# Moving the bias and cache loads, and the stores of new keys and values, from SyncE's DMA queue to GpSimd's, in a two-layer streaming encoder kernel

## The chip, the cores and the metric

The kernel runs on one core of one Trainium2 chip. The core has five engines with a queue of instructions each: TensorE (PE, with its weight loads as PEld), VectorE (DVE), ScalarE (ACT), GpSimd (POOL) and SyncE (SP), and 16 DMA engines that all queues share. An engine starts its instructions in the order in which they are written; an instruction that waits holds up everything behind it on that engine. A DMA is started by an instruction in the queue of some engine. The metric is the device time in microseconds (us) of one execution, the median of several runs.

## What is computed

Two groups of frames share the weights: 256 frames of a new stream and 64 frames that continue an old one. Cut to what matters:

```python
for l in range(DEPTH):                                   # DEPTH = 2
    qa, ka, va, qb, kb, vb, qi, ki, wi = project(x, w_in[l], pos)
    oa = band_attention(qa, ka, va, cache_a_k[l], cache_a_v[l], rel_bias[l])   # bias by clipped distance
    ob = sparse_attention(qb, kb, vb, qi, wi, ki, cache_b_k[l], cache_b_v[l], cache_b_kidx[l])
    x = layer_norm(ALPHA * x + concat(oa, ob) @ w_out[l])
    x = layer_norm(ALPHA * x + relu(x @ w_up[l]) ** 2 @ w_down[l])
# returned: x, and the new ka, va, kb, vb, ki of each layer
```

## The kernel before

All activations lie transposed, features on the partitions and the 320 frames along the row. Each product of fp32 matrices is made of three matmuls on split operands (high by high, high by low, low by high): the helper `mm3`, lines 188 to 190 of the profile. A weight block of 128 by 1024 numbers, a *unit*, is loaded in pairs of 1 MB into one of two `raw` buffers (`load_raw`, L151), split by ACT into its high part `wh` (L170) and by DVE into the low part `wl` (L176). When the second unit of a pair is split, `split_rest` calls `need_raw`, which writes the load of the pair after the next.

The order of the instructions of each engine is fixed in the program: a list of delayed calls (`later`, `advance`, with the delays of the table `WAIT`) decides where attention work stands among the matmuls, and nothing is rescheduled behind it.

In the projection part of a layer, each head pair gets a `Pair` object. Where it is of band A, `bias_tiles` loads its bias first: per head one load of 128x128, one of 128x256 (`bp[h]`) and one of 64x320 (`bs`), all L341; after each head two POOL memsets (L342, L343) mask corners of the tile just loaded, and so wait for the first two of these loads to land. Then `Pair.__init__` clears a piece of the value tile (L364, POOL) and loads cached keys and values (L367, L368). For the sparse branch `Index` loads its cached keys once per layer (L483).

POOL also prepares the queries of the continued stream: `sample_blocks` (L351 copy, L352 and L353 memsets), called when a query has been projected. TensorE's score matmuls for the continued stream read that tile: L535 for the indexer (`dots`), L396 for attention (`scores`). They stand in TensorE's order among the projection matmuls, so what makes them wait makes every matmul behind them wait.

New keys and values are stored to DRAM right after they are computed: `o_ka` (L771), `o_kb` (L308), `o_va` and `o_vb` (L317), `o_ki` (L499). All loads and stores are in SP's queue.

Of the kernel before, what the change touches and what calls it, by code (L numbers as in the profile page):

```python
# [69 lines left out]
def encoder_step(ctx: ExitStack, tc: tile.TileContext, a: dict):  # L70
    nc = tc.nc
# [19 lines left out]
    def main_acc():  # L91
        return acc("mm", 8 - N_SIDE)
# [4 lines left out]
    def side_banks(n, fn, *args):  # L97

        if held[0] + n > N_SIDE:
            later(NEXT, fn, *args)  # L100
            return None
        held[0] += n
        return [acc("at", N_SIDE) for _ in range(n)]

    def release(n):
        held[0] -= n

    def unit(dt=F32, w=T):
        return st([P, 3 * P], "u", N_UNIT, dt)[:, :w]
# [8 lines left out]
    def later(dt, fn, *args):  # L118
        agenda.append((clock[0] + dt, len(agenda), fn, args))
# [161 lines left out]
    def evacuate(dst, src, scale=1.0):  # L281
        s, b = src
        if b is None:
            nc.scalar.activation(dst, s, AF.Copy, scale=scale)
        elif scale != 1.0:
            nc.vector.tensor_scalar(dst, s, b, scale, op0=ALU.add, op1=ALU.mult)
        else:
            nc.scalar.activation(dst, s, AF.Identity, bias=b, scale=scale)

    def swap(dst, src):  # L290
        for q in range(4):
            nc.scalar.activation(dst[32 * q:32 * q + 32], src[32 * (q ^ 1):32 * (q ^ 1) + 32], AF.Copy)  # L292

    def rotate(t, f, sw, c):
        nc.vector.tensor_tensor(t, f, rope[:, c], op=ALU.mult)
        nc.vector.tensor_tensor(sw, sw, rope[:, c + 1], op=ALU.mult)
        nc.vector.tensor_tensor(t, t, sw, op=ALU.add)

    def roped(t, src, c, out, then):

        f, sw = unit(), unit()
        evacuate(f, src)
        swap(sw, f)

        def turn():
            rotate(t, f, sw, c)
            if out is not None:
                nc.sync.dma_start(out, t)  # L308
            then()

        later(WAIT[l]["rope"], turn)

    def value(v, src, out, then):

        f = unit()
        evacuate(f, src)
        nc.sync.dma_start(out, f)  # L317

        def turn():
            got = side_banks(1, turn)  # L320
            if not got:
                return
            pt = got[0]
            release(1)
            for c, n in ((0, P), (1, P), (2, TS)):
                nc.tensor.transpose(pt[:n, c * P:(c + 1) * P], f[:, c * P:c * P + n], ident)
            nc.scalar.activation(v[:, 0:2], pt[:, 0:2 * P].rearrange("p (c d) -> p c d", c=2), AF.Copy)
            nc.scalar.activation(v[:TS, 2], pt[:TS, 2 * P:3 * P], AF.Copy)
            then()

        later(WAIT[l]["value"], turn)

    def bias_tiles(l, j):

        e = a["rel"]
        bp, bs = [unit(w=3 * P) for _ in range(2)], unit()
        for h in range(2):
            off = e.offset + (l * 8 + 2 * j + h) * N_DIST
            for dst, at0, n, m in ((bp[h][:, 0:P], 192, P, P), (bp[h][:, P:], 64, P, 2 * P),
                                   (bs[64 * h:64 * h + 64], 0, TS, NKEY)):  # L340
                nc.sync.dma_start(dst, bass.AP(tensor=e.tensor, offset=off + at0, ap=[[1, n], [1, m]]))  # L341
            nc.gpsimd.memset(bp[h][64:P, 64:P], NEG)  # L342
            nc.gpsimd.memset(bp[h][64:P, 5 * 64:6 * 64], NEG)  # L343
        return bp, bs
# [10 lines left out]
    class Pair:  # L355


        def __init__(self, l, br, j, add):
            self.qf, self.k, self.v = unit(w=3 * P), unit(), unit(w=3 * P).rearrange("p (c d) -> p c d", c=3)
            self.o = unit(F32R), unit(F32R)  # L360
            self.flip = br == "a"
            self.q = self.qf[:, 64:] if self.flip else self.qf[:, :T]
            self.qs = self.qf[:, :P] if self.flip else self.qf[:, 2 * P:]
            nc.gpsimd.memset(self.v[TS:, 2], 0.0)  # L364
            self.add = add
            self.kc, self.vc = unit(w=PAST), unit(w=PAST).rearrange("p (c d) -> p c d", c=2)
            nc.sync.dma_start(self.kc, a["kc" + br][l, j])  # L367
            nc.sync.dma_start(self.vc, a["vc" + br][l, j])  # L368
            self.cols = (slice(192, T), slice(64, 192), slice(0, 64)) if self.flip else (
                slice(0, P), slice(P, 2 * P), slice(TP, T))  # L370
            self.have = set()
            self.done = False
# [58 lines left out]
        def turn(self):  # L431
            banks = side_banks(3, self.turn)
            if not banks:
                return
            release(3)
            self.pt = []
            for h, (p, t) in enumerate(zip((*self.sp, self.ss), banks)):
                pt = unit(w=3 * P)
                if h == 2:
                    nc.gpsimd.memset(pt[TS:, 2 * P:], 0.0)  # L440
                for c, n in ((0, P), (1, P), (2, P if h < 2 else TS)):
                    nc.tensor.transpose(t[:n, c * P:(c + 1) * P], p[:, c * P:c * P + n], ident)  # L442
                if h < WAIT[l]["pa" if self.flip else "pb"]:
                    nc.vector.tensor_copy(pt, t[:, :3 * P])
                elif h < 2:
                    nc.scalar.activation(pt, t[:, :3 * P], AF.Copy)
                else:
                    nc.scalar.activation(pt[:, :2 * P], t[:, :2 * P], AF.Copy)
                    nc.scalar.activation(pt[:TS, 2 * P:], t[:TS, 2 * P:3 * P], AF.Copy)
                self.pt.append(pt)  # L450
            self.got("p")
# [23 lines left out]
    class Index:  # L475


        def __init__(self, l):
            self.l = l
            self.qf = [unit(w=3 * P) for _ in range(4)]  # L480
            self.q = [q[:, :T] for q in self.qf]
            self.kx = unit(w=PAST)
            nc.sync.dma_start(self.kx, a["kidx"][l])  # L483
            self.mask = []
            self.k = self.w = None
            self.weighed = 0
# [9 lines left out]
        def turn(self):  # L496
            self.k = unit()
            rotate(self.k, self.kd, self.sw, 0)
            nc.sync.dma_start(a["o_ki"][self.l], self.k[0:64])  # L499
            self.weights()  # L500

        def weights(self):
# [246 lines left out]
    for l in range(DEPTH):  # L749
# [4 lines left out]
        def take(name, j, src):  # L754
            if name == "ki":
                index.keys(src)
            elif name == "qi":
                roped(index.q[j], src, 0, None, lambda: index.got(j))
            else:
                p, kind, br = pairs[name[1], j], name[0], name[1]  # L760
                if kind == "v":
                    value(p.v, src, a["o_" + name][l, j], lambda: p.got("v"))
                elif br == "b":
                    roped(getattr(p, kind), src, 2 if kind == "q" else 0, a["o_kb"][l, j] if kind == "k" else None,
                          lambda: p.got(kind))
                elif kind == "q":
                    evacuate(p.q, (src[0][:, T - 1::-1], src[1]), scale=HD ** -0.5)
                    later(WAIT[l]["a"] - WAIT[l]["scores"] if kind == "k" else 0, p.got, kind)
                else:
                    evacuate(p.k, src)  # L770
                    nc.sync.dma_start(a["o_ka"][l, j], p.k)  # L771
                    later(WAIT[l]["a"] - WAIT[l]["scores"] if kind == "k" else 0, p.got, kind)

        uses = []
        for s, (name, j) in enumerate(W_IN_ORDER[l]):
            br = name[1]
            if name[1] in "ab" and (br, j) not in pairs:
                pairs[br, j] = Pair(l, br, j, bias_tiles(l, j) if br == "a" else index.mask)
            uses.append(partial(take, name, j))
            if l > 0 or s > 0:  # L780
                project(base + s + 1 - len(uses), l > 0 and s < N_DEFER, *uses)
                uses = []
# [12 lines left out]
        for m in range(KD):  # L795
            if m < N_OUTER:
                p = accs[m]
            else:
                prefetch(wo + m + AHEAD)
                p = main_acc()  # L800
# [26 lines left out]
        for m in range(KD):  # L827
            if m % 2 == 0:
                later(2.0, before.apply, m)
            p = main_acc()  # L830
# [102 lines left out]
```

## Time and profile before

| | us |
|---|---|
| median of 3 runs | 839.5 (838.03 to 839.92) |
| the profiled execution | 836.99 |
| its span, first to last instruction | 835.2 |
| TensorE busy | 821.1 |
| VectorE busy | 594.6 |
| ScalarE busy | 494.0 |
| GpSimd busy | 28.7 |
| mean granted TensorE clock | 0.993 of full speed |

The span is the time from the first to the last instruction of the profiled execution; 1.8 us of its own time lie around it. "Busy" counts work of an engine, not the issuing of DMAs, which stands under the name of the queue (SPq). A granted clock of 1.00 is TensorE's 2.4 GHz, 0.50 its 1.2 GHz.

### The profile page before, as it was taken

Reading aid. Unit: us, or ns where it says so; the run is one execution under the profiler, and the core shown is the slowest. Engines: PE = TensorE matmul, PEld = TensorE weight load, DVE = VectorE, ACT = ScalarE, POOL = GpSimd, SP = SyncE. Lnnn points to the kernel's source line nnn. Section 1 sums busy time; section 2 is a strip of 40 time slices with the busy share of each in tenths; the row PEclk is TensorE's granted clock in tenths of the full one; section 3 lists DMA queues with packets and bytes.
Section 4 is the critical chain, followed back from the end, with each engine's and each line's share of the span. In section 5 each row is a group of like instructions: output and inputs, shape, how many; then the busy total and the mean of one; then the engine's idle time right before and its main releaser. Section 6 shows DMA issues by size and latency. Waiting matters only on the chain.

```text
span 835.2 us, 15008 instructions
## 1 busy us (share of the span) xinstructions
PE 821.1 (98%) x5792; PEld 794.3 (95%) x5792; DVE 594.6 (71%) x1284; ACT 494.0 (59%) x955; POOL 28.7 (3%) x145
## 2 busy tenths in 40 slices
PE   9979999999999999999998999999999999999997
PEld 7969999999999999999998989999999999999995
DVE  5649878586998883545496679996699888545343
ACT  6846798565665553434358977885556655434332
POOL 0110000000000000000000010110000000000000
PEclk9999999999999999999999999999999999999998
DMA  8676343343444444534687324342334444434411
GB/s 275 192 191 180 135 143 126 125 151 103 151 156 147 152 154 149 177 127 155 194 171 261 108 101 135 120 177 74 136 145 151 152 151 152 160 144 152 151 51 64
DMA packets 35033, 124.05 MB, mean 149 GB/s; under 512 B 6033, under 2 KB 21521, under 8 KB 22290
## 3 DMA queue, kind: packets, MB, share of 16 engines
q1 hardware_dynamic: 34962, 123.10, 44.6%
q8 instruction: 46, 0.75, 0.4%
q14 instruction: 25, 0.20, 0.1%
HBM read 116.36 MB, written 6.72 MB: 147 GB/s over the span
## 4 chain that ended last, share of the span: by engine, by line
PE 75%; DVE 10%; ACT 8%; DMA 4%; SPq 1%; issue 1%; ACTq 0%; DVEq 0%
PE mm L188 23%; PE mm L189 23%; PE mm L190 23%; DMA raw<-w_all 4%; DVE wl L176 2%; ACT u L292 2%; ACT wh L170 2%; ACT u L418 1%; DVE u L577 1%; PE at L442 1%; DVE m L575 1%; PE at L394 1%; DVE u L410 1%; PE at L461 1%; PE at L396 1%
## 5 line engine op out<-in xcount | busy, mean ns | idle before, releaser
L188 PE MATMUL mm<-u,wh 128*128 128x320 f32 (+1 forms) x1048 | 328.8, 314 | 0.3 <-ACT wh L227 0.2
L190 PE MATMUL mm<-u,wl 128*128 128x320 f32 (+1 forms) x1048 | 324.0, 309 | 0.4 <-DVE wl L176 0.3
L189 PE MATMUL mm<-u,wh 128*128 128x320 f32 (+1 forms) x1048 | 323.8, 309 | 0.2 <-DVE u L233 0.2
L170 ACT ACTIVATE wh<-raw 128x1024 fp32r<-128x1024 f32 x199 | 209.5, 1055 | 182.9 <-PE mm L189 108.4
L176 DVE TENSOR_TENSOR wl<-raw,wh 128x1024 fp32r<-128x1024 f32 x199 | 241.3, 1217 | 57.8 <-ACT wh L170 57.3
L188 PEld LDWEIGHTS mm<-u,wh 128*128 128x128 f32 (+1 forms) x1048 | 196.8, 188 | 2.1 <-ACT wh L227 1.0
L190 PEld LDWEIGHTS mm<-u,wl 128*128 128x128 f32 (+1 forms) x1048 | 196.5, 187 | 1.6 <-DVE wl L228 0.9
L189 PEld LDWEIGHTS mm<-u,wh 128*128 128x128 f32 (+1 forms) x1048 | 196.9, 188 | 0.4 <-DVE u L233 0.4
L188 PE MATMUL mm<-rh,wh 128*128 128x322 f32 x568 | 177.5, 313 | 0.0
L190 PE MATMUL mm<-rh,wl 128*128 128x322 f32 x568 | 176.2, 310 | 0.0
L189 PE MATMUL mm<-rl,wh 128*128 128x322 f32 x568 | 175.8, 310 | 0.0
L189 PEld LDWEIGHTS mm<-rl,wh 128*128 128x128 f32 x568 | 107.2, 189 | 0.2
L188 PEld LDWEIGHTS mm<-rh,wh 128*128 128x128 f32 x568 | 107.1, 189 | 0.2
L190 PEld LDWEIGHTS mm<-rh,wl 128*128 128x128 f32 x568 | 106.5, 188 | 0.0
L603 DVE SCALAR_TENSOR_TENSOR x<-x,mm 128x320 f32<-128x320 f32 x31 | 15.0, 487 | 78.9 <-PE mm L190 78.9
L292 ACT ACTIVATE u<-u 32x320 f32<-32x320 f32 x104 | 48.7, 469 | 1.8
L270 DVE SCALAR_TENSOR_TENSOR z<-mu,mm 128x320 f32<-128x320 f32 x71 | 38.7, 545 | 12.7 <-PE mm L190 12.7
L811 ACT ACTIVATE z<-z,c 128x320 f32<-128x320 f32 x64 | 35.8, 560 | 16.8 <-DVE z L272 15.8
L418 ACT ACTIVATE u<-u,mx 128x128 f32<-128x128 f32 (+2 forms) x80 | 37.0, 464 | 8.9 <-DVE mx L413 8.9
L605 ACT ACTIVATE rh<-x,ln 128x320 fp32r<-128x320 f32 x24 | 13.5, 563 | 45.4 <-DVE x L603 45.4
L818 DVE TENSOR_TENSOR u<-h,u 128x320 fp32r<-128x320 f32 x64 | 31.5, 492 | 7.2 <-DVE h L817 0.5
L272 DVE TENSOR_TENSOR z<-z,rstd 128x320 f32<-128x320 f32 x71 | 34.9, 492 | 0.0
(135 smaller groups left out, 710.4 us busy)
## 6 DMA issues: line engine op xcount, KB each, us to landing
raw<-w_all SPq DMA_DIRECT2D x99, 1024.0 KB, 4.8
u<-rel SPq DMA_DIRECT2D x16, 128.0 KB, 5.5
u<-rel SPq DMA_DIRECT2D x16, 80.0 KB, 5.8
o_va<-u SPq DMA_DIRECT2D x8, 160.0 KB, 5.3
o_ka<-u SPq DMA_DIRECT2D x8, 160.0 KB, 2.3
o_kb<-u SPq DMA_DIRECT2D x8, 160.0 KB, 1.8
o_vb<-u SPq DMA_DIRECT2D x8, 160.0 KB, 1.8
o_y<-x SPq DMA_DIRECT2D x8, 160.0 KB, 1.9
```

What stands on the lines that cost most here:

```text
L170: nc.scalar.activation(hi, w, AF.Copy)
L176: nc.vector.tensor_tensor(lo, w, hi.bitcast(F32), op=ALU.subtract)
L188: nc.tensor.matmul(out, hi[:, k], xh, start=first, stop=False)
L189: nc.tensor.matmul(out, hi[:, k], xl, start=False, stop=False)
L190: nc.tensor.matmul(out, lo[:, k], xh, start=False, stop=last)
L270: nc.vector.scalar_tensor_tensor(u, mu[:n], p[:, T:T + 1], p[:, :T], op0=ALU.mult, op1=ALU.add)
L272: nc.vector.tensor_tensor(u, u, rstd[:n], op=ALU.mult)
L292: nc.scalar.activation(dst[32 * q:32 * q + 32], src[32 * (q ^ 1):32 * (q ^ 1) + 32], AF.Copy)
L418: nc.scalar.activation(p, p, AF.Exp, bias=self.mx[:, i:i + 1], scale=1.0, accum_out=self.sums[:, i:i + 1])
L603: nc.vector.scalar_tensor_tensor(r, r, ALPHA, psum, op0=ALU.mult, op1=ALU.add)
L811: nc.scalar.activation(u, u, AF.Relu, bias=b)
L818: nc.vector.tensor_tensor(hl, h, hh.bitcast(F32), op=ALU.subtract)
```

## The change

Every DMA of the projection part except the weights moves from SP's queue to POOL's: the bias loads, the cached keys and values, the indexer's cached keys, and the stores of new keys and values. These are 116 DMAs: 48 of the bias, 32 of the attention caches, 2 of the indexer's cache, 34 stores. SP keeps the weights, the inputs, the tables and the result. What is computed, where, and with which buffers stays as it was.

```diff
@@ roped
-                nc.sync.dma_start(out, t)
+                nc.gpsimd.dma_start(out, t)
@@ value
-        nc.sync.dma_start(out, f)
+        nc.gpsimd.dma_start(out, f)
@@ bias_tiles
-                nc.sync.dma_start(dst, bass.AP(tensor=e.tensor, offset=off + at0, ap=[[1, n], [1, m]]))
+                nc.gpsimd.dma_start(dst, bass.AP(tensor=e.tensor, offset=off + at0, ap=[[1, n], [1, m]]))
@@ Pair.__init__
-            nc.sync.dma_start(self.kc, a["kc" + br][l, j])
-            nc.sync.dma_start(self.vc, a["vc" + br][l, j])
+            nc.gpsimd.dma_start(self.kc, a["kc" + br][l, j])
+            nc.gpsimd.dma_start(self.vc, a["vc" + br][l, j])
@@ Index.__init__
-            nc.sync.dma_start(self.kx, a["kidx"][l])
+            nc.gpsimd.dma_start(self.kx, a["kidx"][l])
@@ Index.turn
-            nc.sync.dma_start(a["o_ki"][self.l], self.k[0:64])
+            nc.gpsimd.dma_start(a["o_ki"][self.l], self.k[0:64])
@@ take
-                    nc.sync.dma_start(a["o_ka"][l, j], p.k)
+                    nc.gpsimd.dma_start(a["o_ka"][l, j], p.k)
```

The order of PE, DVE and ACT stays the same to the row. On SP, early in the first layer, the rows between two weight loads leave (`raw` is a weight pair, `u_391` to `u_393` are bias tiles, `u_410` and `u_411` cached keys and values of the first A pair):

```order
 L151 DMA raw_299<-w_all 128x2048
-L499 DMA o_ki<-u_325 64x320
-L341 DMA u_391<-rel 128x128
-L341 DMA u_391<-rel 128x256
-L341 DMA u_393<-rel 64x320
-L341 DMA u_392<-rel 128x128
-L341 DMA u_392<-rel 128x256
-L341 DMA u_393<-rel 64x320
-L367 DMA u_410<-kca 128x256
-L368 DMA u_411<-vca 128x256
 L151 DMA raw_422<-w_all 128x2048
```

The weight pair `raw_422` now stands right behind `raw_299`.

On POOL the same rows come in at the same place of the program, in front of a `sample_blocks` copy of an indexer query (`u_171`). The piece shown begins with the loads of the second head; the three loads and two memsets of the first head stand in front of it in the same form:

```order
+L341 DMA u_392<-rel 128x128
+L341 DMA u_392<-rel 128x256
+L341 DMA u_393<-rel 64x320
 L342 MEMSET u_392 64x64
 L343 MEMSET u_392 64x64
 L364 MEMSET u_406 64x128
+L367 DMA u_410<-kca 128x256
+L368 DMA u_411<-vca 128x256
 L351 COPY u_171<-u_171 64x64
 L352 MEMSET u_171 64x64
 L353 MEMSET u_171 64x64
```

The copy of `u_171` now stands behind eight DMA issues, and the DMAs of the second head and the caches stand behind the memsets that wait for the loads of the first.

In the second layer the A pairs come first, so that four pairs' loads and four stores of values follow each other on POOL ahead of the first query copy of the layer (`u_4836`). This is the end of that stretch:

```order
 L343 MEMSET u_5027 64x64
 L364 MEMSET u_5041 64x128
+L367 DMA u_5045<-kca 128x256
+L368 DMA u_5046<-vca 128x256
+L317 DMA o_va<-u_5057 128x320
+L317 DMA o_va<-u_5116 128x320
 L351 COPY u_4836<-u_4836 64x64
```

Where POOL had 20 memsets ahead of the copy of `u_4836`, counted from the first load of the layer, it now has these and 37 DMA issues: one of the indexer's cache, 24 of bias, 8 of caches and 4 stores.

## Rows read from the trace of the kernel before

**Rows 1.** The page: busy time by engine, share of the span, instructions.

```profile
PE 821.1 (98%) x5792; PEld 794.3 (95%) x5792; DVE 594.6 (71%) x1284; ACT 494.0 (59%) x955; POOL 28.7 (3%) x145
```

**Rows 2.** Timeline of TensorE's weight loads: start, length, instruction, [idle before <-releaser].

```profile
45.47 0.52 PEld L533 LDWEIGHTS at<-u,u 64*128 64x128 f32 x6 [1.93 <-ACT u L541]
...
58.95 1.30 PEld L394 LDWEIGHTS at<-u,u 64*128 64x128 f32 x8 [2.91 <-ACT u L328]
...
449.42 0.52 PEld L394 LDWEIGHTS at<-u,u 64*128 64x128 f32 x8 [2.65 <-ACT u L288]
```

**Rows 3.** Timeline of ScalarE: splits of weights that waited for their load.

```profile
43.98 1.06 ACT L170 ACTIVATE wh<-raw 128x1024 fp32r<-128x1024 f32 x1 [4.97 <-DMA raw<-w_all]
...
57.42 1.06 ACT L170 ACTIVATE wh<-raw 128x1024 fp32r<-128x1024 f32 x1 [8.61 <-DMA raw<-w_all]
...
446.48 1.06 ACT L170 ACTIVATE wh<-raw 128x1024 fp32r<-128x1024 f32 x1 [3.38 <-DMA raw<-w_all]
```

**Rows 4.** Stretches: length, busy by engine, granted clock, DMA share, GB/s.

```profile
8.00:12.00 4.00, 3.70 (x23) 3.05 (x23) 2.98 (x9) 3.17 (x9) 0.00 (x0) 1.00 0.92 316
56.00:72.00 16.00, 13.36 (x74) 11.96 (x72) 12.65 (x45) 10.38 (x26) 0.44 (x3) 0.79 0.58 137
409.00:447.00 38.00, 38.00 (x258) 37.41 (x256) 27.60 (x48) 19.75 (x37) 3.56 (x23) 1.00 0.90 214
440.00:480.00 40.00, 37.61 (x282) 35.34 (x280) 26.25 (x69) 35.62 (x84) 3.29 (x19) 1.00 0.55 186
```

**Rows 5.** Timeline of SP's queue: start of the issue, its length.

```profile
30.86 3.26 SPq L341 DMA_DIRECT2D u<-rel  x6
...
35.95 0.37 SPq L151 DMA_DIRECT2D raw<-w_all  x1
...
48.53 0.36 SPq L151 DMA_DIRECT2D raw<-w_all  x1
...
408.81 0.38 SPq L483 DMA_DIRECT2D u<-kidx  x1
...
439.18 0.38 SPq L151 DMA_DIRECT2D raw<-w_all  x1
```

**Rows 6.** Timeline of VectorE: the splits that free a raw buffer.

```profile
33.00 1.23 DVE L176 TENSOR_TENSOR wl<-raw,wh 128x1024 fp32r<-128x1024 f32 x1 [0.23 <-ACT wh L170]
...
47.28 1.22 DVE L176 TENSOR_TENSOR wl<-raw,wh 128x1024 fp32r<-128x1024 f32 x1
```

**Rows 7.** Timeline of GpSimd: copies and memsets of sample blocks.

```profile
32.83 0.23 POOL L351 COPY u<-u 64x64 f32<-64x64 f32 x1 [3.10 <-DVE u L297]
...
33.31 0.14 POOL L353 MEMSET u<- 64x64 f32 x1
...
443.26 0.36 POOL L351 COPY u<-u 64x64 f32<-64x64 f32 x1 [1.25 <-DVE u L286]
```

**Rows 8.** Timeline of TensorE: score matmuls that read a sample block.

```profile
46.31 0.87 PE L535 MATMUL at<-u,u 128*128 128x256 f32 x4
...
51.87 0.87 PE L535 MATMUL at<-u,u 128*128 128x256 f32 x4
...
450.27 0.73 PEld L396 LDWEIGHTS at<-u,u 128*128 128x128 f32 x4 [0.33 <-issue]
```

**Rows 9.** Timelines of GpSimd and VectorE around 484 us.

```profile
483.91 1.10 POOL L351 COPY u<-u 64x64 f32<-64x64 f32 x1 [9.38 <-DVE u L297]
485.07 0.15 POOL L352 MEMSET u<- 64x64 f32 x1
...
483.69 1.22 DVE L176 TENSOR_TENSOR wl<-raw,wh 128x1024 fp32r<-128x1024 f32 x1
484.83 1.86 DVE L557 SCALAR_TENSOR_TENSOR u<-u,wi,u 128x128 f32<-128x128 f32 x5
```

**Rows 10.** The page's DMA issues: KB each, median us from issue to landing.

```profile
u<-rel SPq DMA_DIRECT2D x16, 128.0 KB, 5.5
...
o_kb<-u SPq DMA_DIRECT2D x8, 160.0 KB, 1.8
```

## Prediction

> **What bounds the kernel now.** I read the page first. TensorE is busy 821.1 of 835.2 us, POOL 28.7 [rows 1]: nothing but TensorE's time can shorten the kernel, and what can lengthen it is whatever makes TensorE wait. So I looked next for its idle time, in the timeline of its weight loads. Three waits stand out: 1.93 us before 45.47, 2.91 before 58.95, 2.65 before 449.42, each ended by ScalarE [rows 2]. ScalarE's timeline says why it was late: each time a split `wh` had waited for its `raw` load, until 43.98, 57.42 and 446.48 [rows 3], and ScalarE's next results freed TensorE. The middle wait cost more than itself: over the stretch from 56 to 72 the granted clock is 0.79 [rows 4], so 0.21 x 16 = 3.4 us of work were lost in it, against none over the stretch around the third wait (1.00). Late weights thus cost 1.9 + 2.9 + 3.4 + 2.65 = 10.9 us at most.
>
> SP's queue shows how late. `raw_422` could go when the split that frees its buffer ended, at 33.00 + 1.23 = 34.23 [rows 6]; it went at 35.95, behind six bias issues (3.26 us from 30.86) and the caches [rows 5], and ScalarE had it 8.0 us after its issue. The load before the second wait left at 48.53 [rows 5], 0.03 after its split (47.28 + 1.22 [rows 6]): that one was not held up by the queue, but by the chain from the first late load, and by the traffic beside it. Before the third wait the load left at 439.18.
>
> **The change, part by part.** *SP loses 116 issues.* Weights go when their buffer is free: 1.7 us sooner at the first place. If nothing else happened, at most the 10.9 us above would come back.
>
> *POOL gains 116 issues, in order with its own work.* What is queued behind them is what counts: the copies of `sample_blocks`, for which the matmuls of L535 and L396 wait in TensorE's order [rows 8], with every projection matmul behind them. The trace has no DMA issued by POOL, so I bound the time c of one issue. The nearest by kind is SP's issue of the same loads: 3.26 / 6 = 0.54 us [rows 5]. The nearest by engine is POOL's own work: 0.23 for a 64x64 copy, but 1.10 for the same copy beside a DVE operation on two SBUF operands (L176, 1.22 us long) [rows 7, 9]. DVE is busy 27.6 of the 38 us in which the second layer's loads run [rows 4], so I take the upper end, **c = 1.0**, and keep 0.54 and 1.5 (an issue of 0.54 that waits out most of a 1.22 us DVE operation) for the range. The Trainium skill (DMA: Bandwidth & Descriptors, Specifications) gives about 1 us to the first byte for DMAs from GpSimd against 0.6 from SyncE; as an estimate the sum by that page would be mine; no run here shows it.
>
> Landing: a store in quiet took 1.8 us from its issue, a bias load 5.5 behind weights in SP's queue [rows 10]. In a queue of its own I take 3.0 from the start of the issue, near the quiet end.
>
> One A pair on POOL then takes 8 issues (8.0), plus twice the wait of the memset L343 for the second of three loads (its landing 2.0 after its issue's end, of which the third issue covers 1.0: 1.0 left, so 2.0), plus five memsets (0.8): **10.8 us**, where it was a pair of short bursts. In general 6c + 4.8.
>
> *First layer.* POOL is free at 33.31 + 0.14 = 33.45 [rows 7]. Pair one ends at 44.25, and the copy of `u_171` with its memsets (32.83 to 33.45, 0.62 [rows 7]) at 44.9. L535 reads it: it ran at 46.31 [rows 8], and without the first late weight would have run at 46.31 - 1.93 = 44.4. So TensorE waits 0.5 and is 1.4 us earlier than before. Pair two ends at 55.7, the copies of `u_404` and `u_170` at 56.9. L535 wants `u_170` at 51.87 - 1.4 = 50.5 [rows 8] and waits 6.4: now 5.0 late. The second weight wait is absorbed (2.9 back), but not the fall of the clock, since a longer idle time stands before it: net **+2.1 us**. For the later A pairs of this layer TensorE asks further apart; I count nothing.
>
> *Second layer.* The first issue, at 408.81 [rows 5], is set by buffers that TensorE frees, so it stays. One issue to 409.8, four pairs 43.2, four stores 4.0: 457.0, and `u_4836` at 457.6, where it was copied at 443.26 [rows 7]. L396 wants it at 450.27 - 2.65 = 447.6 [rows 2, 8] with weights on time. TensorE waits 10.0: +7.3 against 450.27. So long a pause I charge with a fall of the clock like that of the first layer, 3.4: **+10.7 us**.
>
> *Start.* The indexer's cached keys (128 KB) now leave at about 1.5 us, beside the inputs for which TensorE waits; at 316 GB/s [rows 4] they take **+0.4**.
>
> The other 30 stores, and the cache loads of the sparse pairs, stand one to three at a time between POOL's copies: nothing, since POOL is idle for 806 us of the span [rows 1]; without that cover each would cost its 1.0.
>
> Sum: 2.1 + 10.7 + 0.4 = +13.2 us. The profiled execution took 836.99, so 850.2; the median of the runs is 2.5 above it, so **853 us**.
>
> **Does DVE hold POOL's issues?** The copy at 483.91 took 1.10 instead of 0.23 beside DVE's two-operand work, and the memset at 485.07 only 0.15, though a two-operand DVE row (484.83, five instructions) ran beside it [rows 9]: POOL is held where it reads, not where it only writes. The Trainium skill (SBUF — State Buffer, Who interferes with whom) says the same of two SBUF inputs, and names DVE's two-port modes as what shuts POOL out altogether; its section on the two separate sides of SBUF says that descriptors for POOL's DMAs cannot be written meanwhile. By that, as an estimate, c would stay near 1 in the second layer's stretch, where DVE does mostly two-operand work; by the copy's row it would go to 1.5.
>
> **The rivals.**
>
> *POOL issues as fast as SP (faster).* c = 0.54: a pair takes 8.0. `u_171` is ready at 42.1, no wait; `u_170` at 51.3, 0.6 before 51.87 (-0.6); the second wait goes with its clock fall (-2.9 - 3.4); in the second layer `u_4836` is ready at 444.2, before 447.6 (-2.65). Sum -9.5 + 0.4 = -9.1: 830 us. For it: POOL has nothing else to do [rows 1]. Against: 0.54 is below what POOL needs for one copy beside DVE. It decides below c = 0.75, where a pair takes 9.3, `u_170` costs 2.0 (2.9 back) and `u_4836` comes at 450.4, as today.
>
> *Issues are held, or loads land late (much slower).* c = 1.5: a pair takes 13.8; `u_171` at 47.9, `u_170` at 62.9, 11.0 late, 8.1 after the absorbed wait; `u_4836` at 472.1, 21.8 late plus 3.4 of clock. Sum +34: 873 us. A landing after 5.5 us instead of 3.0 would, at c = 1.0, do as much (5 us per pair, 20 in the second layer, 10 in the first: +43).
>
> *No change.* What matters is the traffic, not the queue: at the second wait the weights had left at once and still came late [rows 3, 5], because bias rows and 2 MB of weights shared the DMA engines. If POOL's loads only interleave, weights stay late and hide POOL's delay: 839.5. The Trainium skill (DMA: Bandwidth & Descriptors, Issuing engines are not separate DMA queues) states this: all issuers run on the same 16 DMA engines and only issue time is saved. Against it stands the second layer, where POOL's 49 us from its first issue to `u_4836` have to fit into 39.
>
> **How the numbers follow.** Forecast 0.55, with its own range 847 to 863 (c from 0.85 to 1.25: +7.1 and +23.6); much slower 0.20; POOL as fast as SP 0.15; no change, or a gain and a loss that cancel at c near 0.75, 0.10. Within 0.2% is 837.8 to 841.2, about what runs of this kernel can tell. Faster: 0.15 + 0.02 = 0.17; same 0.06; slower 0.55 + 0.20 + 0.02 = 0.77. The range leaves out most of the fast rival (below 835, about 0.1) and the upper part of the slow one (above 876, under 0.1): 835 to 876.
>
> **What would show it.** Right: in the changed trace POOL's issues take about 1 us each; the weight loads leave within 0.1 us of their split; TensorE waits for POOL at an L535 near 51 to 57 (about 6 us) and at an L396 near 448 to 458 (about 10 us), with a granted clock of 0.50 for some us behind each; no wait of ScalarE for `raw` ends a TensorE wait there. Wrong: POOL's issues of 0.7 us or less, or loads landing within 2 us, would leave only gains; issues of 1.5 us, or memsets waiting 4 us for their loads, would take it past 870. Were L396 of the second layer to start at 447 while POOL is still issuing, my chain through `sample_blocks` would be false.

## The result, and the profile after

The changed kernel takes **862.98 us** (median of 4 runs, 860.98 to 863.37), the kernel before 838.76 in the same comparison: a ratio of 1.0293, 95% interval 1.0259 to 1.0327, so 24.2 us slower. The profiled executions have spans of 835.2 and 860.9 us, with mean granted clocks of 0.993 and 0.978.

The page and the DMA view of the changed kernel answer to [rows 1] and [rows 10]. The first line is busy time by engine, the next two are the queues (SP's, then POOL's: packets, MB, share of 16 engines), the last three are DMA issues (KB each, median us to landing).

```profile
PE 828.6 (96%) x5792; PEld 800.0 (93%) x5792; DVE 595.2 (69%) x1284; ACT 494.0 (57%) x955; POOL 91.8 (11%) x261
...
q1 hardware_dynamic: 19410, 108.77, 36.0%
q0 software_dynamic: 5024, 14.33, 8.9%
...
u<-rel POOLq DMA_DIRECT2D x16, 128.0 KB, 5.5
...
o_kb<-u POOLq DMA_DIRECT2D x8, 160.0 KB, 2.2
...
u<-kca POOLq DMA_DIRECT2D x8, 128.0 KB, 2.6
```

TensorE is 7.5 us longer busy (its mean granted clock is lower) and, since the span grew by 25.7, idle 18.2 us more. The timeline of its weight loads shows where (answers to [rows 2]).

```profile
50.30 1.36 PEld L535 LDWEIGHTS at<-u,u 128*128 128x128 f32 x4 [4.67 <-POOL u L353]
64.49 1.35 PEld L535 LDWEIGHTS at<-u,u 128*128 128x128 f32 x4 [6.94 <-POOL u L353]
96.98 0.73 PEld L396 LDWEIGHTS at<-u,u 128*128 128x128 f32 x4 [1.51 <-POOL u L353]
215.44 0.19 PEld L188 LDWEIGHTS mm<-rh,wh 128*128 128x128 f32 x1 [1.82 <-issue]
471.08 1.35 PEld L396 LDWEIGHTS at<-u,u 128*128 128x128 f32 x4 [12.23 <-POOL u L353]
```

Before, all three long waits ended at ScalarE; now the long ones end at line 353, the last memset of `sample_blocks`. Why that memset was late is in the chain of work from 28 to 70 us (start, length, what):

```profile
34.60 0.52 POOL u L341
35.12 6.12 DMA u<-rel
41.24 0.05 issue
41.28 0.15 POOL u L343
41.43 0.51 POOL u L341
41.94 6.29 DMA u<-rel
48.23 0.05 issue
48.28 0.15 POOL u L343
48.42 0.14 POOL u L364
48.56 0.52 POOL u L367
49.08 0.54 POOL u L368
49.62 0.26 POOL u L351
```

One head's bias has to land (6.12 us) before its mask, the mask before the next head's issue, and that head's bias (6.29) before the caches' issues and the copy that TensorE waits for. Of the 15.1 us from the first issue (34.55 in POOL's timeline) to the copy, 12.4 are two loads in flight, one after the other. The waits by engine count this up for the whole program (total us, times, longest):

```profile
POOL u L342 <- DMA u<-rel: 46.8, 16, 5.1
...
POOL u L343 <- DMA u<-rel: 24.2, 14, 3.1
```

The issues themselves are short: the view of the array `rel` gives min/median/max in ns of all 48.

```profile
L341 POOL DMA_DIRECT2D u<-rel x48: 530/536/571, 34.6 to 463.2; - x48
```

In the second layer the stretch in question of POOL's timeline begins at the first line below and reaches the copy of `u_4836` (the second line) 55.9 us later:

```profile
414.53 1.62 POOL L341 DMA_DIRECT2D u<-rel  x3 [208.34 <-PE mm L190]
...
470.42 0.23 POOL L351 COPY u<-u 64x64 f32<-64x64 f32 x1
```

And while TensorE stands still from 459, its granted clock falls to 0.50, which is 1.2 GHz (columns as in [rows 4]):

```profile
460.00:464.00 4.00, 0.00 (x0) 0.00 (x0) 0.91 (x6) 0.73 (x1) 1.91 (x5) 1.00 0.95 359
464.00:468.00 4.00, 0.00 (x0) 0.00 (x0) 0.00 (x0) 0.78 (x2) 0.43 (x3) 0.54 0.76 121
468.00:472.00 4.00, 0.91 (x2) 0.82 (x3) 0.00 (x0) 0.00 (x0) 3.47 (x9) 0.50 0.41 148
472.00:476.00 4.00, 4.00 (x21) 3.71 (x21) 2.82 (x5) 2.41 (x3) 1.10 (x4) 0.68 0.24 86
476.00:480.00 4.00, 4.00 (x29) 3.96 (x28) 0.21 (x1) 3.93 (x14) 0.00 (x0) 1.00 0.64 223
```

How far TensorE is behind the kernel before at the same instruction gives the loss by stage: 0.25 us at 21, 9.6 at the first layer's L631 (196.88, now 206.44), 11.4 at the second L631 (420.49, now 431.85), 20.8 at the second layer's L396 (450.27, now 471.08), 21.9 at the third L631 (597.73, now 619.59), 25.7 at the end. So the first layer costs 9.3, the second 9.5, the stretch between them 1.8, the rest 1.1 and the tail 3.8. These are figures of one execution, and the first layer's is known to some 3 us only: in two kernels further down that differ from the changed one in the second layer alone (four and twelve added memsets), the first L631 comes at 203.79 and 204.49 instead of 206.44.

The 1.8 were unforeseen. The second layer's indexer keys and its first three bias loads were already issued at 198, not near 409 with the rest, beside a weight load that ScalarE then waited 2.91 us for (timelines of POOL and ACT); TensorE's wait before 215.44 is behind it. From the first L631 to the second it takes 225.4 us, where the kernel before takes 223.6; so does, with the same loads on POOL at 190.49, the kernel with shifted rows below, whose loads land sooner.

```profile
198.47 0.54 POOL L483 DMA_DIRECT2D u<-kidx  x1 [33.34 <-PE mm L189]
199.00 1.59 POOL L341 DMA_DIRECT2D u<-rel  x3
...
209.12 1.06 ACT L170 ACTIVATE wh<-raw 128x1024 fp32r<-128x1024 f32 x1 [2.91 <-DMA raw<-w_all]
```

### The profile page after: what moved, and what is told of

Same layout as the page of the kernel before. It is cut to its first block, busy times and chain, and to the rows that moved or that the text cites. A ratio compares the mean times of both kernels' runs of the same rounds, so it can differ in the third digit from the quotient of the medians.

```text
span 860.9 us, 15029 instructions
## 1 busy us (share of the span) xinstructions
PE 828.6 (96%) x5792; PEld 800.0 (93%) x5792; DVE 595.2 (69%) x1284; ACT 494.0 (57%) x955; POOL 91.8 (11%) x261
## 3 DMA queue, kind: packets, MB, share of 16 engines
q0 software_dynamic: 5024, 14.33, 8.9%
## 4 chain that ended last, share of the span: by engine, by line
PE 68%; DVE 10%; DMA 9%; ACT 7%; POOL 3%; issue 2%; SPq 0%; POOLq 0%; ACTq 0%; DVEq 0%
PE mm L188 21%; PE mm L190 21%; PE mm L189 21%; DMA u<-rel 6%; DVE wl L176 2%; DMA raw<-w_all 2%; ACT u L292 2%; ACT u L418 1%; DVE u L577 1%; ACT wh L170 1%; DVE m L575 1%; PE at L461 1%; DVE u L410 1%; PE at L442 1%; DVE x L645 1%
## 5 line engine op out<-in xcount | busy, mean ns | idle before, releaser
L176 DVE TENSOR_TENSOR wl<-raw,wh 128x1024 fp32r<-128x1024 f32 x199 | 241.5, 1218 | 58.8 <-ACT wh L170 58.5
L341 POOL DMA_DIRECT2D u<-rel x48 | 25.7, 540 | 209.2 <-PE mm L190 208.3
L270 DVE SCALAR_TENSOR_TENSOR z<-mu,mm 128x320 f32<-128x320 f32 x71 | 38.7, 545 | 12.2 <-PE mm L190 12.1
L410 DVE CUSTOM_DVE_ANT_0 u<-at,u 128x128 f32<-128x128 f32 (+2 forms) x80 | 25.8, 380 | 23.6 <-PE at L396 12.1
```

What stands on the lines that cost most here:

```text
L176: nc.vector.tensor_tensor(lo, w, hi.bitcast(F32), op=ALU.subtract)
L270: nc.vector.scalar_tensor_tensor(u, mu[:n], p[:, T:T + 1], p[:, :T], op0=ALU.mult, op1=ALU.add)
L341: nc.gpsimd.dma_start(dst, bass.AP(tensor=e.tensor, offset=off + at0, ap=[[1, n], [1, m]]))
L410: nc.vector.tensor_tensor_reduce(dst, s, add, scale=1.0, scalar=-3.0e38, op0=ALU.add, op1=ALU.max, accum_out=self.mx[:, i:i + 1])
```

## The experiments

**Theory 1**: the loss is order on POOL, that is masks that wait for bias loads, with DMAs and query copies behind them. **Rivals**: the number of issues on POOL; the traffic; the price of the masks anywhere. Ratios are to the kernel before in the same comparison; for the first four kernels it took 837.73 us.

**Masks late.** On top of the change, the four masking memsets of a pair go behind its query copy, in `Pair.got`:

```diff
-            nc.gpsimd.memset(bp[h][64:P, 64:P], NEG)              # in bias_tiles
-            nc.gpsimd.memset(bp[h][64:P, 5 * 64:6 * 64], NEG)
+                if self.flip:                                      # in Pair.got, behind sample_blocks
+                    for t in self.add[0]:
+                        nc.gpsimd.memset(t[64:P, 64:P], NEG)
+                        nc.gpsimd.memset(t[64:P, 5 * 64:6 * 64], NEG)
```

> All 116 DMAs stay on POOL; the four masking memsets of a pair's bias tiles, which wait for two of three bias loads of each head to land, move from right behind those loads to right behind the pair's query copy. Theory 1 (the loss is POOL waiting in order for bias loads to land, in front of the query copies that TensorE needs): a pair takes 8 x 0.54 us of issues instead of 12 to 16 us, no query copy is late, the weights leave on time: 828 to 838 us, at or below the kernel before (838.8). Rival 1 (the issues themselves, 116 x 0.54 us, are the cost): stays above 855. Rival 2 (the moved loads share the DMA engines with the weights and make these late): 839 to 848, with TensorE waiting behind ScalarE splits that wait for weights.

Measured: 833.34, ratio 0.9951 (0.9932 to 0.9969). The whole loss is gone, with all 116 DMAs still on POOL, and after the first 2 us no wait of TensorE over 0.4 us ends at POOL any more. POOL's timeline now has the copies of the first two pairs at 38.24 and 47.26, where the change alone had them at 49.61 and 63.14:

```profile
33.70 3.26 POOL L341 DMA_DIRECT2D u<-rel  x6
37.00 0.20 POOL L362 MEMSET u<- 64x128 f32 x1
37.15 0.57 POOL L365 DMA_DIRECT2D u<-kca  x1
37.71 0.54 POOL L366 DMA_DIRECT2D u<-vca  x1
38.24 0.56 POOL L349 COPY u<-u 64x64 f32<-64x64 f32 x1
...
47.26 1.14 POOL L349 COPY u<-u 64x64 f32<-64x64 f32 x1
```

**Bias back on SP.** The change without its 48 bias loads:

```diff
-                nc.gpsimd.dma_start(dst, bass.AP(tensor=e.tensor, offset=off + at0, ap=[[1, n], [1, m]]))
+                nc.sync.dma_start(dst, bass.AP(tensor=e.tensor, offset=off + at0, ap=[[1, n], [1, m]]))
```

> The changed kernel with the 48 bias loads back on SP's queue; the 68 other DMAs stay on POOL. Theory 1: POOL's issues no longer stand behind one another's landings as much, but POOL's memsets still wait for the bias loads from SP, and SP's weights stand behind bias issues again: 838 to 842 us. Rival 1: 68 of 116 issues remain, so 14 of the 24 us: about 853. Rival 2: caches and stores are little traffic: about 839.

Measured: 830.23, ratio 0.9921 (0.9899 to 0.9943): the loss is gone as theory 1 says, but the kernel is also 8 us faster than expected. The three waits of [rows 2] are gone, and SP's queue shows how: with stores and caches out of it, nothing that waits for a result stands ahead of the bias loads. In the first layer they go at 28.86 instead of 30.86 [rows 5], and the weights behind them at 35.20 instead of 35.95. In the second layer they go at 401.60, but this is no gain of the queue: TensorE is 7.2 us ahead by then (its second L631 is at 413.28), and 7.2 before 408.81 is the same place. There the weights behind them gain: those that went at 439.18 go at 430.80, 1.2 us sooner than that lead alone would give. At the second layer's L396 the kernel is 9.7 us ahead of the kernel before (440.61), of the 10.9 that the prediction set as the most that late weights cost.

```profile
28.86 3.23 SPq L341 DMA_DIRECT2D u<-rel  x6
35.20 0.34 SPq L151 DMA_DIRECT2D raw<-w_all  x1
...
401.60 3.12 SPq L341 DMA_DIRECT2D u<-rel  x6
```

**Loads of both heads first.** All six loads of a pair, then its four masks, on POOL:

```diff
-            nc.gpsimd.memset(bp[h][64:P, 64:P], NEG)
-            nc.gpsimd.memset(bp[h][64:P, 5 * 64:6 * 64], NEG)
+        for t in bp:
+            nc.gpsimd.memset(t[64:P, 64:P], NEG)
+            nc.gpsimd.memset(t[64:P, 5 * 64:6 * 64], NEG)
```

> The changed kernel with all six bias loads of a pair issued before its four memsets, instead of three loads, two memsets, three loads, two memsets. Theory 1: one wait for landing per pair instead of two, some 5 us less per pair; the 6.9 us wait at the fourth indexer query and the 12.2 us wait at the first query of the second layer shrink to near nothing: 840 to 850 us. Rival 1: same issues, 863. Rival 2: bias traffic comes in larger lumps beside the weights: 863 or more.

Measured: 843.95, ratio 1.0079 (1.0057 to 1.0102). POOL's waits for the bias fall from 71 us to 37. Overlapping the two landings of a pair gives back three quarters of the loss. Of the rest TensorE's weight loads show 4.71 us at an L535 and 1.90 at the second layer's L396, both for POOL, where landings still stand ahead of the copy, and 2.78 for ScalarE just before that L396. In the second layer's stretch POOL waits 18.9 us for landings and 7.4 in front of a store of values, until VectorE's L646.

**Other rows.** Bias tiles filled from other arrays (cached keys, rotary table), whose rows, or pieces of rows, don't overlap; the bias values are not the reference's.

```diff
-            for dst, at0, n, m in ((bp[h][:, 0:P], 192, P, P), (bp[h][:, P:], 64, P, 2 * P),
-                                   (bs[64 * h:64 * h + 64], 0, TS, NKEY)):
-                nc.gpsimd.dma_start(dst, bass.AP(tensor=e.tensor, offset=off + at0, ap=[[1, n], [1, m]]))
+            kc = a["kca"][l, j]
+            for dst, src in ((bp[h][:, 0:P], kc[:, 0:P]), (bp[h][:, P:], kc),
+                             (bs[64 * h:64 * h + 64], a["rope"][64 * h:64 * h + 64, 0])):
+                nc.gpsimd.dma_start(dst, src)
```

> The changed kernel with the bias loads taken from other arrays of the same widths, in which each partition's row is a row of its own and aligned, instead of rows of one table that start 4 bytes apart; the bias values are wrong by this, all work is done. It tells why bias loads take about 5 us to land on POOL where cache loads take 2.6. If the form of the rows does it, landing falls to about 2.6 us, POOL's waits from 71 to some 30 us, and the time to 840 to 850 us. If it is the queue or the weights beside them, landing stays near 5 and the time near 863.

Measured: 843.06, ratio 1.0062 (1.0042 to 1.0082). The 128 KB loads (with the eight loads of cached keys among them) land after 2.9 us instead of 5.5, POOL waits 39 us instead of 71, and TensorE waits once in each layer for POOL, 7.16 and 4.93 us. That the bias loads are slow by their own form, not by the queue, makes most of the loss.

**Rows shifted, but apart.** Which part of that form? Here the cached keys are read with one element between rows, so that each row's start moves on by 4 bytes against whole rows, as with the real bias rows, but none overlaps (bias values again not the reference's):

```diff
-                nc.gpsimd.dma_start(dst, bass.AP(tensor=e.tensor, offset=off + at0, ap=[[1, n], [1, m]]))
+                kc = a["kca"]
+                nc.gpsimd.dma_start(dst, bass.AP(tensor=kc.tensor, offset=kc.offset + at0, ap=[[m + 1, n], [1, m]]))
```

> The changed kernel with the bias tiles loaded from the array of cached keys (wrong bias values, same tile shapes and queue), each row behind the row before it with one element between them: the rows don't overlap, but each starts 4 bytes further past a boundary, as the real bias rows do. If the overlap of the real rows makes their landing slow, it lands as with whole rows of that array (2.9 us for 128 KB, 2.6 for 64 KB) and the time is 841 to 847. If the odd start of each row does, it lands after 5 to 6 us as in the changed kernel, and the time is 859 to 866.

Measured: 842.19 (the kernel before: 838.67), ratio 1.0039 (1.0019 to 1.0059). From its page and DMA view: POOL's queue, and the loads of 128 KB (with the eight cache loads among them) and 64 KB:

```profile
q0 software_dynamic: 5024, 14.33, 5.3%
...
u<-kca POOLq DMA_DIRECT2D x24, 128.0 KB, 3.3
...
u<-kca POOLq DMA_DIRECT2D x16, 64.0 KB, 2.3
```

The same 5024 packets and 14.33 MB take 5.3% of the DMA engines' time instead of 8.9%. So the odd start of a row is not what is slow. What is left is that the 128 rows, each shifted by one element, come out of one stretch of 1.0 to 1.5 KB. (That the bias array's own place in memory matters beside it is not excluded.)

For the next four kernels the kernel before took 837.21.

**The masks late, without the change** (the first diff above, applied to the kernel before):

> The kernel before, all DMAs on SP, with the four masking memsets of a pair moved behind the copy of that pair's query. It is the control for the run with masks late on top of the change. Theory 1 (the loss is the order on POOL: memsets that wait for bias loads stand ahead of DMAs and query copies) expects no change here, since in the kernel before no TensorE wait ended at POOL: 835 to 840. Rival (the late masks are a gain by themselves, and the change's own price was not in POOL's order): 830 to 834, that is the same -0.5% as with the change.

Measured: 839.31, ratio 1.0016 (0.9995 to 1.0038). The place of the masks is free while the loads are on SP; it is the change that makes it matter.

**Only the bias on POOL** (the diff of "bias back on SP" the other way round, on the kernel before):

> The kernel before with only the 48 bias loads on POOL; caches, indexer keys and stores stay on SP. Theory 1: nearly the whole loss is there without the other 68 issues, since the memsets wait for the same landing of 5 us: 852 to 863, POOL waiting 60 to 75 us in L342 and L343, TensorE waiting for POOL at an L535 near 50 to 65 and at an L396 near 455 to 475. Rival (the number of issues on POOL makes the loss, 48 of 116 of it): 846 to 850. Rival (loads alone are harmless, stores waiting for DVE stand in front): 836 to 840.

Measured: 851.1, ratio 1.0182 (1.0146 to 1.0217): 13.9 of the 24 us, just under the range of theory 1 and above that of its rival. The trace splits it by layer. The first layer loses 9.0 us (L631 at 205.87), as with the whole change: the bias loads alone make it, by waits of 6.55 and 5.73 us at the two L535. The second layer loses only 1.0 (L396 goes from 9.9 to 10.9 us behind), because POOL reaches the copy of `u_4836` 47.5 us after its first load of the stretch instead of 55.9, and TensorE comes hardly earlier:

```profile
461.20 1.35 PEld L396 LDWEIGHTS at<-u,u 128*128 128x128 f32 x4 [1.43 <-POOL u L353]
```

There the twelve issues of caches and stores (12 x 0.54 = 6.5 us) make up most of the 8.4 us between the two, on top of a chain that just fits. So theory 1 alone explains the first layer; in the second the number of issues, the rival's term, counts as well. That is read from these two traces; no run takes it apart further.

**Bias on SP and masks late:**

> Caches, indexer keys and stores on POOL, bias loads on SP, and the masks behind the query copies. With the bias on SP no POOL wait held TensorE any more (830.2 before, against 833.3 for masks late with the bias on POOL), so theory 1 expects that the masks' place no longer matters: 828 to 832. Rival (POOL's memsets still delay something behind them, the caches or query copies): 822 to 827.

Measured: 831.67, ratio 0.9939 (0.9919 to 0.996), as theory 1 expected; not told apart from 0.9921 for the bias on SP alone.

**Only the stores on POOL:**

```diff
-                nc.sync.dma_start(out, t)       # and the other three lines of stores
+                nc.gpsimd.dma_start(out, t)
```

> The kernel before with only the 34 stores on POOL; all loads stay on SP. If what the change has to give is that loads on SP no longer stand behind stores which wait for VectorE's results (bias loads of the second layer then go at about 402 instead of 409, the first ones 2 us earlier), the stores alone give most of the gain: 830 to 834. Rival (the gain comes from cache loads and the indexer's keys leaving SP's queue, so that weights go sooner): 836 to 839. Rival (stores on POOL wait for VectorE and hold query copies behind them): 842 to 850.

Measured: 835.29, ratio 0.9972 (0.9954 to 0.9989), a third of what the bias on SP brought, and between the first two expectations. TensorE still waits 1.55 us near 56 and 1.77 near 443 for ScalarE; the rest of the gain needs the caches out of SP's queue too. The profiled execution reads better than the median: at the third L631 it is 6.5 us ahead of the kernel before, against 8.2 with the bias on SP, and loses 3.7 of that in the tail.

The last runs ask whether POOL's chain alone sets the second layer's L396 (the kernel before: 838.25, and 837.57 for the run with twelve memsets).

**More work on POOL**, four memsets of a whole value tile (0.46 us each) in each A pair of the second layer, and **three times as much**, twelve:

```diff
+            if l == 1 and self.flip:
+                for _ in range(4):              # 12 in the second run
+                    nc.gpsimd.memset(self.v, 0.0)
```

> The changed kernel plus four memsets of a whole value tile (128x384) on POOL in each of the second layer's four A pairs, between the bias loads and the cache loads. Theory 1: in the second layer POOL's own time from 414 to 470 sets TensorE's L396, so the added time counts one for one: at an estimated 0.4 to 0.6 us each (a 64x128 memset took 0.20) 16 of them are 6 to 10 us; L396 starts near 477 to 481 and the time is 868 to 874. Rival (what sets L396 is when the loads land, and added work hides in those waits, or the price is that of traffic): 862 to 865, L396 near 471.

Measured with four: 861.55, ratio 1.0282 (1.0259 to 1.0305): no slower than the change alone, the rival's number. 7.4 us of work were added, but from POOL's first load of the stretch to the copy of `u_4836` it took 58.4 us instead of 55.9: the waits of L342 and L343 had shrunk from 33.5 to 28.9. That even these 2.5 don't show in the time is chance: in the profiled execution TensorE was 2.9 us ahead of the changed kernel already at the second L631 (428.98), where nothing had been added, and the tail was 3.1 shorter.

> As with four memsets of a value tile per A pair of the second layer, but twelve: 22.2 us of added POOL work there at the 0.46 us each that the run with four showed. With four, 7.4 us were added and only 2.5 arrived, since the memsets' waits for bias loads fell from 33.5 to 28.9 us. Theory 1, corrected (POOL's chain sets L396, but added work first uses up waits for landings): a head's two waits can hardly fall below 3.2 us together, 22 for the seven heads waited for, so at most 11 of the 22.2 hide, L396 starts near 480 to 490 and the time is 870 to 884. Rival (L396 is set by something beside POOL's chain, such as weights, and work on POOL costs nothing): 860 to 865.

Measured with twelve: 879.47, ratio 1.0506 (1.0475 to 1.0537), some 17 us slower than the change alone. POOL adds 22.7 us, the copy comes 75.6 us after the first load instead of 55.9, and TensorE waits for it:

```profile
488.18 1.35 PEld L399 LDWEIGHTS at<-u,u 128*128 128x128 f32 x4 [20.11 <-POOL u L353]
```

So POOL's chain does set L396, as corrected theory 1 said, but a little added work is not paid one for one: the waits of L342 and L343 come to 33.5 us without it, 28.9 with four memsets and 31.1 with twelve. That the loads, issued at another moment beside the weights, land sooner or later is the likely reason, not a shown one. The added memsets have a second path as well: they write the value tile, so ScalarE waits for them where it fills that tile (L327, 9.58 us before 465.15), and TensorE waits 11.65 us before 467.14 behind it. It does not set L396, which POOL's copy releases later.

**The change in the first layer alone** (each moved line picks the queue by the layer, `nc.sync if l else nc.gpsimd`):

> The change for the first layer alone: DMAs of the second layer's projection stay on SP, among them the bias loads issued near 198. Theory 1 (first layer 9 to 10 of the 24, second layer 9 to 11, early loads at 198 under 2): 846 to 850, TensorE waiting for POOL at the two L535 near 50 and 64 and nowhere else. Rival (first layer's delay is made good later, since attention work fills TensorE's later waits, and the second layer sets the whole): 838 to 842.

Measured: 846.39, ratio 1.0093 (1.0073 to 1.0114). TensorE waits for POOL at the two L535 (4.70 and 6.28 us) and otherwise only 1.00 us at an L396 near 97, where the whole change had 1.51; and what the first layer lost is not made good later. By the medians it is 8.1 us of the 24, and the other 16 belong to the second layer's DMAs; the profiled execution, the longest of its six, ends 12.6 behind. TensorE is 9.25 us behind at the first L631 and 9.25 at the second, so the 1.8 between them is gone together with the loads at 198 on POOL.

## Why the prediction was right in its direction and its place, and which terms were mis-sized

The time lies at the very upper end of the prediction's own range, 847 to 863, and the loss is nearly twice the forecast 13.2. That it lies inside is luck: two terms were off by nearly a factor of two each, in opposite directions.

**The mechanism** held. TensorE waits at the two L535 and the L396 that were named, for `sample_blocks` behind bias loads on POOL; the weights leave SP's queue at once (35.40, where the split that frees the buffer ended at 34.15 + 1.23 = 35.38); and the second wait for weights is gone. Taking the masks from between loads and copies removes the loss; that is shown by the first experiment and its control.

**"c = 1.0"** was wrong by nearly a factor of two: 0.54, as SP's first six in [rows 5]. **"In a queue of its own I take 3.0"** for the landing was wrong the other way: 5.5, as in SP's queue [rows 10]. The two errors cancelled in part. With the measured values, the landing counted from the start of the issue, a head waits 5.5 - 2 x 0.54 = 4.4 us for its second load, and a pair takes 8 x 0.54 + 2 x 4.4 + 0.8 = 13.9 us; the trace has 12.4 to 16.2, against 10.8 forecast. The row that said so stood in [rows 10]; the prediction set it aside because weights were in front of the loads in that queue. The experiment with rows apart shows that it is the load's own form.

**"POOL's issues of 0.7 us or less ... would leave only gains"** was therefore false: that bound varied c with a short landing, and the slow rival (+43 for 5.5) held c at 1.0. Each condition was named alone; the pair that occurred was not. And even with landings of 2.9 to 3.3 and c = 0.54, in the two kernels with other rows, the time was 0.4 to 0.6% above that of the kernel before, not the fast rival's 830. Here the general form "6c + 4.8" slipped: it keeps the landing 2.0 us behind the end of its issue, so that a smaller c makes the landing sooner too. With 3.0 from the start of the issue, as the prediction has it, it is 4c + 6.8, and the fast rival's pair takes 9.0 us instead of 8.0; the first pair of the kernel with shifted rows took 9.0 (34.07 to 43.07), the second 12.1, and the waits of a head came to 2.3 us (37.4 over 16 heads). In the second layer a store of values that stands ahead of bias loads also waited 6.23 us (o_va at 428.49 in the kernel with shifted rows, released by VectorE's L646).

**First layer, "+2.1"**: +9.3. Pairs of 15.1 and 12.9 us make the first L535 wait too (4.67, forecast 0.5) and the second 6.94 (forecast 6.4); and the clock fell behind each of them. The mean granted clock is 0.79 over 40 to 56 as over 56 to 72; before, that fall stood in the second of these stretches alone [rows 4].

```profile
40.00:56.00 16.00, 11.49 (x63) 10.45 (x62) 8.67 (x19) 6.15 (x12) 5.79 (x18) 0.79 0.79 169
56.00:72.00 16.00, 9.46 (x54) 8.13 (x53) 6.03 (x21) 4.17 (x9) 7.25 (x22) 0.79 0.63 119
```

**Second layer, "+10.7"**: +9.5, nearly right, but by other parts. "Set by buffers that TensorE frees, so it stays" was right in its first half only: POOL's first load of the stretch moves with TensorE. It goes 17.3 us before TensorE's second L631, at 414.53 in the changed kernel, and also in kernels in which TensorE comes earlier (the first line below is of the kernel with four added memsets, the second of that with shifted rows, L631 at 428.98 and 422.08):

```profile
411.66 1.62 POOL L341 DMA_DIRECT2D u<-rel  x3 [208.33 <-PE mm L190]
404.75 1.62 POOL L342 DMA_DIRECT2D u<-kca  x3 [210.54 <-PE mm L190]
```

For a TensorE on time that is 403.2, not 408.81: the loads stood at 408.81 because of SP's queue. So the first layer's delay moves POOL's stretch and TensorE alike, and the second layer's loss comes on top of it in full. POOL starts 5.6 us sooner than forecast and takes 55.9 us, not 49, which leaves a wait of 12.23 instead of 10.0. The 3.4 charged for the clock came to 1.1 at most, the rest up to the third L631. The pair of 13.9 us alone would have been the slow rival's 13.8, whose sum was +34; the sooner start, a head whose loads were out at 198 and the cheaper clock, none of them foreseen, kept it to 24.

**Start, "+0.4"**: 0.25 in this execution. The kernel before has that instruction at 20.88, and with late masks but all DMAs on SP at 20.37, so differences of this size are not resolved.

**Left out**: the loads issued at 198 (+1.8) and the tail (+3.8). The tail is no part of the change: from the third L631 to the end it lasts 241.3 us after and 237.5 before, but 238.2 in the kernel with four added memsets, which has the same DMAs, and 241.2 in that with only stores on POOL. It goes with the granted clock at the end: over the stretch from 228 to 236 us behind the third L631 that is 0.79 before and 0.71 with four added memsets, but 0.50 after and with only stores on POOL.

**Does DVE hold POOL's issues?** It was the prediction's reason for c = 1.0, and no: in 48 issues the longest is 571 ns, and the twelve that ran beside L176 took 530 to 571 as the others did, while the copy at 47.26 in the kernel with late masks, beside L176, took 1.14 us as in [rows 9]. The trace agrees with the Trainium skill (SBUF — State Buffer, Who interferes with whom) that two SBUF inputs hold POOL's reading; no run here shows an issue held. The prediction's "near 1" was a guess on top of that rule, not worked out from it.

**"No change"**, the rival, is what follows from the rule that issuing engines are not separate queues (the Trainium skill, DMA: Bandwidth & Descriptors, Issuing engines are not separate DMA queues). The trace agrees for the landing of the bias, 5.5 us from either queue. By that rule the change would have been worth nothing, and the 2.9% show what it leaves out: what stands behind the DMA in its engine's order. Other moved loads did land sooner. The cached keys took 5.6 us from SP's queue before, 2.6 from POOL's after, and 4.5 from POOL's with the bias back on SP, so what goes beside them or before them counts as well; no run takes these apart:

```profile
u<-kca SPq DMA_DIRECT2D x8, 128.0 KB, 5.6
...
u<-kca POOLq DMA_DIRECT2D x8, 128.0 KB, 4.5
```

The fit in the Trainium skill (DMA: Bandwidth & Descriptors, Anatomy of one DMA — SWDGE (gpsimd) path), 2.0 us plus bytes over 436 GB/s, gives as an estimate 2.3 us for 128 KB. The cached keys come near it in the changed kernel (2.6); the bias loads do not (5.5), and with their rows apart they come nearer (2.9 to 3.3).

## What to carry to other kernels

When a load moves to another engine's queue, count not its issue but what on that engine waits for its landing, and what stands behind that wait: here a 0.15 us mask held a 0.23 us copy for a whole landing, and putting the mask behind the copy turned +2.9% into -0.5%. Move what nobody on the new engine waits for (caches and stores gave -0.8%) and leave the rest. If two unknown sizes enter one sum, price the corner in which each goes its own way, and try a landing time from the row of the same load first: here it held for the bias loads (5.5 us from either queue), but not for the cached keys (5.6 against 2.6).

## What was not expected of the hardware

- An issue of a bias load on POOL takes 530 to 571 ns over all 48, of 128 or of 64 rows, beside VectorE's L176 or not. On SP the same 48 took 328 to 833 ns, 472 in the median.
- Loads whose 128 rows overlap, each shifted by one element, take nearly twice as long as loads of the same shapes from another array, whose rows lie apart: 5.5 us against 3.3 (128 KB), 4.5 against 2.3 (64 KB), and 8.9% against 5.3% of the DMA engines' time for POOL's queue.
- The same bytes are fewer packets on POOL's queue: 24434 packets on both queues after, against 34962 on SP's alone before, without a faster landing of the bias.
- Work added to an engine that waits for loads is not paid one for one: 7.4 us cost 2.5, 22.7 cost 19.7, measured at the copy behind it.
